# Output projection of a streaming-encoder block in a seven-product form, on eight cores

## The chip, the cores and the metric

One Trainium2 chip, all 8 of its cores, each working on its own eighth of the tokens. The metric is the device time of the slowest core in microseconds (us). A program on all eight cores has a second, slower state in some of its executions, in which the cores of a die show a lower granted clock of the matrix engine (TensorE); such runs are called slow here and are kept out of every comparison. A ratio sets the fast runs of one kernel against the fast runs of the kernel before, both taken in the same rounds on the same chip. It can differ by some 0.1% from the ratio of the means or medians of the times that are quoted.

## The reference

One layer: two token mixers side by side, one output projection of their joined outputs, then a squared-ReLU MLP of four times the width. D_MODEL is 1024, D_FF 4096, and there are 4 x 8192 tokens, so 4096 per core.

```python
def reference(x, ...):
    h = rmsnorm(x, norm1_g[l])
    p = jnp.einsum('bsd,de->bse', h, w_in[l])          # b_gate, c_gate, xc, u, v: 512 columns each
    # ... cut: mixer A, a gated width-3 convolution -> y_a ; mixer B, chunk-causal spatial gating -> y_b
    y = jnp.concatenate([rmsnorm(y_a, ...), rmsnorm(y_b, ...)], axis=-1)
    x = x + jnp.einsum('bse,ed->bsd', y, w_out[l])     # <- the output projection, 1024 x 1024
    h2 = rmsnorm(x, norm2_g[l])
    a = jax.nn.relu(jnp.einsum('bsd,df->bsf', h2, w_up[l]))
    x = x + jnp.einsum('bsf,fd->bsd', a * a, w_down[l])
    return rmsnorm(x, final_g)
```

## The kernel before

Each core handles eight tiles of MT = 512 tokens. The first stage ("mixing", about 70 to 430 us) goes through the eight tiles; the second ("expansion and contraction", 430 to 1220 us) runs the MLP on four groups of two tiles, with its weights streamed through six ring buffers. Between them lies what this text calls the passage: the last tile's mixing is interleaved with the first expansion matmuls. A small list scheduler in the kernel's own source orders all instructions of all engines when the program is built, from assumed costs, and the hardware then runs each engine's queue in that fixed order.

Expansion and contraction already use a seven-product (Strassen-Winograd) form: two halves of outputs by two halves of inputs by two halves of tokens take seven products instead of eight, for which sums of weights (on VectorE, "PREP" tiles, stored to DRAM during mixing) and sums of tokens are needed. The output projection did not: it took 8 groups of 8 matmuls of 512 columns a tile, and VectorE added each finished bank to the residual X.

```python
        def y_norm(src, q, ebase):               # YN: normalised mixer outputs, fp16, [8 x 128 inputs, 512 tokens]
            rs = RS[nxt("rs", 3)]
            rstd(rs[:, :], stats(src, q, 4, ONESE), MT, rs.keys())
            for c in (0, 2):
                tt(YN[:, ebase + c:ebase + c + 2, :], src[:, c:c + 2, :], rs[...].broadcast_to(...), ALU.mult, ...)

        def out_proj(m):
            b = X[(m + 1) % 3]
            for dc in range(8):
                bank = bank8()
                for e0 in (0, 4):
                    pe(bank, [(bank[:, :], WO[:, e_, dc * 128:(dc + 1) * 128], YN[:, e_, :], e_ == 0, e_ == 7)
                              for e_ in range(e0, e0 + 4)], YN.keys(e0, 4) + WO.keys(0, 8))
                tt(b[:, dc, :], bank[:, :], b[:, dc, :], ALU.add, bank.keys() + b.keys(dc), b.keys(dc))
                if dc % 2:                       # store two finished rows of the residual
                    ...
            rs = RS[nxt("rs", 3)]                # norm factors of the sum, stored for the MLP
            rstd(rs[:, :], stats(b, X1Q, 8, ONESD), MT, rs.keys())
            dma("sp", rs_d[m], rs[:, :], rs.keys(), ...)

        # ... cut: the order of a tile
            y_norm(YA, SQ[0], 0)
            if last:
                h2_part(0, 1)                    # MLP inputs H of tile 1 (the first group is tiles 0 and 1), and sums
                h2_sums()
                refill(4)                        # first loads of MLP weights into the ring
            for c in range(4):
                stage_su(m, c)                   # gating
```

Of the kernel before, what the change touches and what calls it, by code (L numbers as in the profile page):

```python
# [17 lines left out]
MT = 512  # L18
# [48 lines left out]
class Sched:  # L67
# [44 lines left out]
    def schedule(self, phys, rounds=8):  # L112


        base = [(op, op.deps) for op in self.ops]
        best = None
        for _ in range(rounds + 1):
            for op, deps in base:
                op.deps = deps
                for b in op.banks:  # L120
                    b.left = len(b.ops)
            order = self.place([op for op, _ in base], phys)
            est = max(o.finish for o in order)
            if best is None or est < best[0]:
                best = (est, order, [(o, o.deps) for o in order],
                        [(o.opens, o.opens.phys) for o in order if o.opens is not None],
                        {o: (o.start, o.finish) for o in order})
            self.push(order, est)
        self.est_total, self.ops = best[:2]
        for o, deps in best[2]:  # L130
            o.deps = deps
            o.start, o.finish = best[4][o]
        for b, p in best[3]:
            b.phys = p
        self.by_eng = {e: [o for o in self.ops if o.eng == e] for e in ENGS}
# [42 lines left out]
    def place(self, ops, phys, lat=0.12, dma_lat=2.0, dma_rate=290e3):  # L178
# [67 lines left out]
        assert len(order) == len(ops)  # L246
# [73 lines left out]
def build_program():  # L320
# [23 lines left out]
    with es:  # L344
# [23 lines left out]
        SQ = [ar.buf(f"SQ{i}", (o + 68 + 4 * i) * KB, [4, MT], BF16) for i in range(2)]  # L368
        HT = [ar.buf("HT0", (o + 126) * KB, [8, MT], F16), ar.buf("HT1", (o + 76) * KB, [8, MT], F16)]
        PREP = [ar.buf(f"PREP{i}", (o + 84 + 7 * i) * KB, [7, 4, 128], F16) for i in range(2)]  # L370
        VH = ar.buf("VH", (o + 98) * KB, [4, MT], F16)
        CT = [ar.buf(f"CT{i}", (o + 102 + 2 * i) * KB, [MT], F32) for i in range(2)]
        T2 = [ar.buf(f"T2{i}", (o + 106 + 2 * i) * KB, [MT], F32) for i in range(2)]
        X = [ar.buf(f"X{i}", (o + a) * KB, [8, MT], F32) for i, a in enumerate((134, 110, 150))]
        WO = ar.buf("WO", (o + 166) * KB, [8, 1024], F16)
        YN = ar.buf("YN", (o + 182) * KB, [8, MT], F16)
        RS = [ar.buf(f"RS{i}", (o + 190 + 2 * i) * KB, [MT], F32) for i in range(3)]
        XQ = [ar.buf("XQ0", (o + 126) * KB, [8, MT], BF16), ar.buf("XQ1", (o + 76) * KB, [8, MT], BF16)]
        X1Q = ar.buf("X1Q", (o + 182) * KB, [8, MT], BF16)
# [8 lines left out]
        RSL = [ar.buf(f"RSL{i}", (o + 196 + 2 * i) * KB, [MT], F32) for i in range(2)]  # L388
# [7 lines left out]
        HQ = [ar.buf("HQ0", (o + 106) * KB, [8, HW], BF16), ar.buf("HQ1", (o + 108) * KB, [8, HW], F16)]  # L396
        SQH, HH = HQ[0][:, :, :], HQ[1][:, :, :]
        WSB = [ar.buf(f"WSB{i}", (o + 84 + 2 * i) * KB, [MT], F32) for i in range(3)]
# [30 lines left out]
        def act(out, in_, func, reads, writes, n=MT, **kw):  # L429
            aps = sum(1 for v in kw.values() if not isinstance(v, (int, float)))  # L430
            S.add("act", lambda e: e.activation(out=out, in_=real(in_), func=func, **kw), reads=reads, writes=writes,  # L431
                  occ=(n / 1.2 + 200 + 70 * aps) / 1000, banks=[in_.bank] if isinstance(in_, Late) else [])

        def dve(fn, reads, writes, n=MT, rate=1, src=None):
            S.add("dve", fn, reads=reads, writes=writes, occ=(n / rate + 151) / 960,
                  banks=[src.bank] if isinstance(src, Late) else [])
# [71 lines left out]
        def stage0_norm(m, bank, step=4):  # L508
            rs = RS[nxt("rs", 3)]
            rstd(rs[:, :], bank, MT, rs.keys())  # L510
            for k in range(0, 8, step):
                normalize(HT[m % 2], X[(m + 1) % 3], rs, k, step)
# [35 lines left out]
        def stage_conv(m, c):  # L548
# [7 lines left out]
            ct = CT[nxt("ct", 2)]  # L556
            act(ct[:, :], bC[:, :], AF.Identity, bC.keys(), ct.keys())
            tt(Z[:, c, 128:640], bX[:, :], ct[:, :], ALU.mult, bX.keys() + ct.keys(), Z.keys(c))
# [7 lines left out]
        def stage_su(m, c):  # L566
            h = HT[m % 2]
            bS, bU = bank8(), bank8()
            pe(bS, [(bS[64 * hh:64 * hh + 64, t * 128:(t + 1) * 128],
                     VH[:, t, (2 * c + hh) * 64:(2 * c + hh + 1) * 64], WST[:, 2 * c + hh, :], True, True)  # L570
                    for t in range(4) for hh in range(2)], VH.keys(0, 4) + WST.keys(0, 8))
            pe(bU, [(bU[:, :], WU[:, k, c * 128:(c + 1) * 128], h[:, k, :], k == 0, k == 7) for k in range(8)],
               h.keys(0, 8) + WU.keys(0, 8))
            t2 = T2[nxt("t2", 2)]
            bias_b = BIAS[:, c, :].unsqueeze(1).broadcast_to([128, 4, 128])
            stt(t2[:, :].rearrange("p (t i) -> p t i", t=4), bS[:, :].rearrange("p (t i) -> p t i", t=4),
                pcol(GLN, c), bias_b, ALU.mult, ALU.add, bS.keys() + [("BIAS",)] + CONST, t2.keys())
            tt(YB[:, c, :], bU[:, :], t2[:, :], ALU.mult, bU.keys() + t2.keys(), YB.keys(c))

        def y_norm(src, q, ebase):  # L580
            rs = RS[nxt("rs", 3)]
            rstd(rs[:, :], stats(src, q, 4, ONESE), MT, rs.keys())
            for c in (0, 2):
                tt(YN[:, ebase + c:ebase + c + 2, :], src[:, c:c + 2, :],
                   rs[:, :].unsqueeze(1).broadcast_to([128, 2, MT]), ALU.mult, src.keys(c, 2) + rs.keys(),
                   YN.keys(ebase + c, 2), n=2 * MT)

        def out_proj(m):
            b = X[(m + 1) % 3]
            for dc in range(8):  # L590
                bank = bank8()
                for e0 in (0, 4):
                    pe(bank, [(bank[:, :], WO[:, e_, dc * 128:(dc + 1) * 128], YN[:, e_, :], e_ == 0, e_ == 7)
                              for e_ in range(e0, e0 + 4)], YN.keys(e0, 4) + WO.keys(0, 8))
                tt(b[:, dc, :], bank[:, :], b[:, dc, :], ALU.add, bank.keys() + b.keys(dc), b.keys(dc))
                if dc % 2:
                    j = dc // 2
                    dst = x1_d[m, :, 2 * MT * j:2 * MT * (j + 1)].rearrange("p (k t) -> p k t", k=2)
                    dma("sp", dst, b[:, 2 * j:2 * j + 2, :], b.keys(2 * j, 2), [("x1", m, j)], ("xs", (m + 1) % 3, j),
                        4 * 128 * 2 * MT)  # L600
            rs = RS[nxt("rs", 3)]
            rstd(rs[:, :], stats(b, X1Q, 8, ONESD), MT, rs.keys())
            dma("sp", rs_d[m], rs[:, :], rs.keys(), [("rsd", m)], ("rss", m % 2), 4 * 128 * MT)

        def combine(p, dst, src, dkeys, reads, margin):
# [4 lines left out]
            tt(p[:, 4, :, :], p[:, 3, :, :], p[:, 2, :, :], ALU.add, p.keys(2, 2), p.keys(4), rate=2)  # L610
            tt(p[:, 3:6:2, :, :], p[:, 0:1, :, :].broadcast_to([128, 2, 4, 128]), p[:, 3:5, :, :], ALU.subtract,
               p.keys(0) + p.keys(3, 2), p.keys(3) + p.keys(5), n=1024, rate=2)
            tt(p[:, 6, :, :], p[:, 1, :, :], p[:, 5, :, :], ALU.add, p.keys(1) + p.keys(5), p.keys(6), rate=2)
# [5 lines left out]
        def prep(i, n):  # L619
            combine(PREP[n % 2], ws(i), wup_d if i < 16 else wdn_d, (i, ("pl", n % 2), ("ps", n % 2)), WO.keys(4) if n < 2 else [], 5.0)  # L620
# [99 lines left out]

        def down_unit(o_, s0, s1):
            bA, bC, bD = banks_acd()

# [11 lines left out]
            d1, d2 = o_, o_ + 4  # L735
            prod(bA, P1, True, False)
            addr(0, d1, bA)
            prod(bD, P2, True, True)
            addr(0, d1, bD)
            prod(bC, P5, True, False)  # L740
            addr(1, d2, bC)
            prod(bA, P6, False, False)
            addr(1, d1, bA)
            prod(bC, P3, False, True)
            addr(1, d1, bC)
            prod(bA, P7, False, False)
            addr(1, d2, bA)
            prod(bA, P4, False, True)
            addr(0, d2, bA)

        def final(g):

            rss = []
            for h in range(2):
                b, rs = R[h], RS[nxt("rs", 3)]
# [99 lines left out]
        for j in range(2):  # L855
            wload(WO[:, 4 * j:4 * j + 4, :], wo_d[j].rearrange("p (k n) -> p k n", k=4), WO.keys(4 * j, 4), ("o", j),
                  2048 * KB)
            gain(lambda k_: WO[:, k_, :], WO, range(4 * j, 4 * j + 4), GCONV, 1024)
# [45 lines left out]
        for m in range(NMT):  # L904
# [16 lines left out]
            y_norm(YA, SQ[0], 0)  # L921
            if last:
                h2_part(0, 1)
                h2_sums()
# [5 lines left out]
            y_norm(YB, SQ[1], 4)  # L930
# [138 lines left out]
```

## Time and profile before

| | |
|---|---|
| time, median of 3 | 1246.82 us (1246.3 to 1248.05) |
| span of the slowest core (core 7) | 1244.9 us |
| TensorE busy / idle | 1209.6 / 35.3 us |
| VectorE busy | 893.4 us |

The head of the page of the kernel before, and its first part: busy time, share of the span and instructions of each engine (PE is TensorE, PEld its weight loads, DVE is VectorE, ACT is ScalarE).

```profile
span 1244.9 us, 18564 instructions; the slowest of 8 cores (1235.7 to 1244.9 us)
...
PE 1209.6 (97%) x5880; PEld 548.5 (44%) x5880; DVE 893.4 (72%) x1377; ACT 530.4 (43%) x905; POOL 86.0 (7%) x146
```

The table by stage (windows) of the kernel before. After the window in us come its length, the busy time of each engine with its number of instructions, then the granted clock, the busy share of the DMA engines and their rate.

```profile
core 7: us, PE busy (x) PEld busy (x) DVE busy (x) ACT busy (x) POOL busy (x), PEclk, DMA share, GB/s
80.00:120.00 40.00, 40.00 (x199) 18.04 (x197) 33.96 (x49) 23.73 (x42) 2.32 (x4) 1.00 0.69 173
120.00:160.00 40.00, 40.00 (x199) 18.06 (x197) 29.39 (x46) 21.25 (x36) 2.13 (x4) 1.00 0.75 192
...
360.00:400.00 40.00, 40.00 (x211) 18.03 (x210) 33.20 (x45) 18.65 (x37) 3.70 (x7) 1.00 0.64 179
400.00:440.00 40.00, 40.00 (x211) 18.01 (x209) 34.28 (x49) 16.44 (x25) 3.73 (x7) 1.00 0.84 266
440.00:480.00 40.00, 40.00 (x187) 18.10 (x186) 29.52 (x43) 24.31 (x40) 6.80 (x10) 1.00 0.70 215
480.00:520.00 40.00, 40.00 (x187) 18.14 (x186) 33.23 (x61) 13.23 (x24) 3.19 (x6) 1.00 0.92 210
```

TensorE works 40.00 of 40.00 us in all of these windows at a granted clock of 1.00: everything else is hidden behind it. The 35.3 us of idle time lie in the load ramp and in the tail.

### The profile page before, as it was taken

The numbers are of one execution on the slowest core, as the hardware profiler recorded it, in microseconds if no ns is written. First come the engines' busy times: TensorE is split into PE (matmuls) and PEld (weight loads), VectorE is DVE, ScalarE is ACT, GpSimd is POOL, SyncE is SP. The second block draws the span as 40 slices with busy tenths as digits, with TensorE's granted clock in tenths as the row PEclk, the third lists the DMA queues.
The fourth block names the chain that finished last, engine by engine and source line by source line (L and its number), as shares of the span: only waits on it lengthen the run. The fifth ranks groups of instructions, "written<-read, shape, count | busy, mean of one in ns | idle before, by whom it ended". The sixth has DMA issues, their size and how long they took to land.

```text
span 1244.9 us, 18564 instructions; the slowest of 8 cores (1235.7 to 1244.9 us)
## 1 busy us (share of the span) xinstructions
PE 1209.6 (97%) x5880; PEld 548.5 (44%) x5880; DVE 893.4 (72%) x1377; ACT 530.4 (43%) x905; POOL 86.0 (7%) x146
## 2 busy tenths in 40 slices
PE   5899999999999999999999999999999999999994
PEld 3444444444444444444444444444444444444442
DVE  2778687877878887658759737767846876855746
ACT  4544655536554356026127205317405406503524
POOL 0100000000001011000101200000110000110000
PEclk9899999999999999999999999999999999999998
DMA  8968688596675869975577764576984645985423
GB/s 185 171 148 232 167 228 231 148 245 175 179 220 153 279 213 207 237 266 176 169 260 228 262 212 162 211 237 177 295 272 148 216 165 182 279 271 177 149 90 135
DMA packets 55183, 253.81 MB, mean 204 GB/s; under 512 B 6192, under 2 KB 6320, under 8 KB 54832
## 3 DMA queue, kind: packets, MB, share of 16 engines
q1 hardware_dynamic: 35152, 180.27, 42.8%
q0 software_dynamic: 19936, 72.36, 25.3%
q8 instruction: 49, 0.80, 0.3%
q14 instruction: 46, 0.38, 0.1%
HBM read 211.71 MB, written 65.01 MB: 222 GB/s over the span
## 4 chain that ended last, share of the span: by engine, by line
PE 93%; DMA 5%; DVE 1%; issue 0%; SPq 0%; DVEq 0%; POOLq 0%
PE PS L424 93%; DMA WSB_109<-bsf 2%; DMA X_74<-xT 1%; DMA X_73<-xT 1%; DMA WV<-wv 1%; DMA WCXB_53<-wcxb 1%; DVE RA L439 0%; DVE RB L439 0%; SPq L450 0%; DVE WU L446 0%; DVEq L344 0%; DVE FSQ_102 L439 0%; DVE FSQ_101 L439 0%; DVE Z L439 0%; DVEq L284 0%
## 5 line engine op out<-in xcount | busy, mean ns | idle before, releaser
L439 DVE TENSOR_TENSOR RB<-PS,RB 128x512 f32<-128x512 f32 x128 | 87.4, 690 | 91.4 <-PE PS L424 88.9
L424 PE MATMUL PS<-YN,WO 128*128 128x512 f16 x512 | 113.8, 379 | 0.0
L439 DVE TENSOR_TENSOR RA<-PS,RA 128x512 f32<-128x512 f32 x96 | 66.1, 690 | 60.6 <-PE PS L424 59.2
L439 DVE TENSOR_TENSOR A_89<-A_89 128x512 bf16<-128x512 bf16 (+1 forms) x192 | 94.5, 508 | 8.2 <-ACT A_89 L431 3.6
L431 ACT ACTIVATE SN_92<-PS 128x512 f32<-128x512 f32 x63 | 37.4, 595 | 106.5 <-PE PS L424 104.7
L424 PEld LDWEIGHTS PS<-YN,WO 128*128 128x128 f16 x512 | 50.1, 98 | 60.4
L424 PE MATMUL PS<-A_89,RING_83 128*128 128x512 bf16 x308 | 76.1, 379 | 0.0
L424 PE MATMUL PS<-A_89,RING_85 128*128 128x512 bf16 x308 | 76.1, 379 | 0.0
L424 PE MATMUL PS<-A_89,RING_86 128*128 128x512 bf16 x308 | 75.8, 379 | 0.0
L424 PE MATMUL PS<-A_89,RING_84 128*128 128x512 bf16 x308 | 75.5, 379 | 0.0
L424 PE MATMUL PS<-H_96,RING_87 128*128 128x512 f16 x308 | 75.1, 379 | 0.0
L424 PE MATMUL PS<-H_96,RING_83 128*128 128x512 f16 x308 | 74.5, 379 | 0.0
L424 PE MATMUL PS<-H_96,RING_88 128*128 128x512 f16 x308 | 74.3, 379 | 0.0
L424 PE MATMUL PS<-H_96,RING_84 128*128 128x512 f16 x308 | 74.3, 379 | 0.0
L431 ACT ACTIVATE SN_90<-PS 128x512 f32<-128x512 f32 x66 | 39.2, 595 | 76.7 <-PE PS L424 75.6
L424 PE MATMUL PS<-A_89,RING_88 128*128 128x512 bf16 x280 | 69.4, 379 | 0.0
L424 PE MATMUL PS<-A_89,RING_87 128*128 128x512 bf16 x280 | 69.1, 379 | 0.0
L431 ACT ACTIVATE SN_93<-PS 128x512 f32<-128x512 f32 x64 | 38.2, 596 | 71.8 <-PE PS L424 71.3
L424 PE MATMUL PS<-H_96,RING_85 128*128 128x512 f16 x280 | 67.9, 379 | 0.0
L424 PE MATMUL PS<-H_96,RING_86 128*128 128x512 f16 x280 | 67.4, 379 | 0.0
L431 ACT ACTIVATE SN_91<-PS 128x512 f32<-128x512 f32 x63 | 37.5, 595 | 70.1 <-PE PS L424 68.0
L439 DVE TENSOR_TENSOR SN_92<-PS,SN_92 128x512 f32<-128x512 f32 x63 | 43.4, 690 | 27.4 <-PE PS L424 22.7
(231 smaller groups left out, 2029.2 us busy)
## 6 DMA issues: line engine op xcount, KB each, us to landing
RING_83<-ws_s SPq DMA_DIRECT2D x21, 896.0 KB, 6.0
RING_84<-ws_s SPq DMA_DIRECT2D x21, 896.0 KB, 6.4
RING_87<-ws_s SPq DMA_DIRECT2D x20, 896.0 KB, 5.3
RING_88<-ws_s SPq DMA_DIRECT2D x20, 896.0 KB, 6.2
RING_85<-ws_s SPq DMA_DIRECT2D x19, 896.0 KB, 6.0
RING_86<-ws_s SPq DMA_DIRECT2D x19, 896.0 KB, 6.3
ws_s<-PREP_65 SPq DMA_DIRECT2D x12, 896.0 KB, 6.3
ws_s<-PREP_66 SPq DMA_DIRECT2D x12, 896.0 KB, 5.6
```

Of the source, the lines that this page charges most:

```text
L424: ins = e.matmul(real(o_), lhsT=l, rhs=r, start=st, stop=sp, skip_group_check=True)
L431: S.add("act", lambda e: e.activation(out=out, in_=real(in_), func=func, **kw), reads=reads, writes=writes, occ=(n / 1.2 + 200 + 70 * aps) ...
L439: dve(lambda e: e.tensor_tensor(out=out, in0=real(in0), in1=in1, op=op), reads, writes, n, rate, in0)
```

## The change

The output projection takes the seven-product form too, over halves of outputs (512), of inputs (512, which are the two mixers) and of the tile's tokens (256). A product is 4 x 2 matmuls of 256 columns, and two 128-wide output chunks share a bank of 512. That makes 2 x 7 x 8 = 112 matmuls of 256 columns a tile instead of 64 of 512: seven eighths of the arithmetic. Its cost: 14 additions of 2 x 256 columns a tile instead of 8 of 512, three sums over the tokens a tile, three sums over the weights once. Weights grow from 16 to 28 KB a partition, tokens from 8 to 14 KB; SBUF was full, so several buffers now lie on top of others. VH now shares memory with RSL, for which a part of the first MLP inputs H (those of tile 1, built during the last tile) comes after the gating instead of before it. The scheduler got a random search of 90 tries; it now assumes that VectorE and ScalarE are occupied for less time by an instruction, and that the result comes later. The diff, cut to its core:

```diff
-    def schedule(self, phys, rounds=8):
+    def schedule(self, phys, rounds=8, tries=90):
...
+            if t:
+                for o, k in best[5].items():
+                    o.key = k if o.fixed else k + rnd.gauss(0, 0.3)
...
-            S.add("dve", fn, reads=reads, writes=writes, occ=(n / rate + 151) / 960,
+            S.add("dve", fn, reads=reads, writes=writes, occ=(n / rate + 65) / 960,
+                  dur=(n / rate + 237) / 960, ...)
...
         def out_proj(m):
-            b = X[(m + 1) % 3]
-            for dc in range(8):
-                bank = bank8()
-                for e0 in (0, 4):
-                    pe(bank, [(bank[:, :], WO[:, e_, dc * 128:(dc + 1) * 128], YN[:, e_, :], e_ == 0, e_ == 7)
-                              for e_ in range(e0, e0 + 4)], YN.keys(e0, 4) + WO.keys(0, 8))
-                tt(b[:, dc, :], bank[:, :], b[:, dc, :], ALU.add, bank.keys() + b.keys(dc), b.keys(dc))
+            x = X[(m + 1) % 3]
+            half = MT // 2
+            for dc in (0, 2):
+                def prod(bank, p, first, last):
+                    a, b = p
+                    pe(bank, [(bank[:, half * u:half * (u + 1)], WO[:, a, k, (dc + u) * 128:(dc + u + 1) * 128],
+                               YN[:, b, k, :], first and u == 0 and k == 0, last and k == 3)
+                              for u in range(2) for k in range(4)],
+                       YN.keys(b) + WO.keys(a))
+                def add(h, d_, bank):
+                    v = x[:, d_:d_ + 2, half * h:half * (h + 1)]
+                    tt(v, bank[:, :].rearrange("p (u t) -> p u t", u=2), v, ALU.add, ...)
+                winograd(prod, add, dc)          # seven products, seven additions; a bank is added to again after it was read
...
-        RS = [ar.buf(f"RS{i}", (o + 190 + 2 * i) * KB, [MT], F32) for i in range(3)]
+        RS1 = [ar.buf(f"RS1{i}", (o + 104 + 2 * i) * KB, [MT], F32) for i in range(3)]
+        RS2 = [ar.buf(f"RS2{i}", (o + 190 + 2 * i) * KB, [MT], F32) for i in range(3)]
...
             y_norm(YA, SQ[0], (3, 2))
             if last:
-                h2_part(0, 1)
-                h2_sums()
                 refill(4)
             for c in range(4):
                 stage_su(m, c)
+            if last:
+                h2_part(0, 1)
+                h2_sums()
+            y_norm(YB, SQ[1], (4, 1))
+            tsum(lambda i, j, d: YN[:, i:j:d, :, :], lambda j: YN.keys(j), 2 * MT)
```

## The prediction

> **What bounds the kernel now.** TensorE. The 40 us windows of the slowest core (span 1244.9 us) show it busy 40.00 of 40.00 us in every window from 80 to 1200 us; its idle time (1244.9 - 1209.6 = 35.3 us) lies in the load ramp before about 69 us and the tail after 1227 us. The chain of waits is 93% matmuls. Granted clock is 1.00 from 80 to 1200 us. A matmul record lasts 379 ns but they are pipelined: 48 output-projection matmuls in a row took 10.52 us in the timeline, a step of (10520-379)/47 = 215.8 ns.
>
> **Removed.** 512 matmuls of 512 columns become 896 of 256 (7/8 of the arithmetic). The timeline has 52 warm-up matmuls of 128 columns, each with its own 128x128 weight load, in 3.07 us, 56 ns a step; a line through 56 ns at 128 and 215.8 at 512 gives 109 ns at 256 (an estimate). That agrees with the Trainium skill, "TensorE: Matmul & The Clock Gate", section "Wait — 56ns, not 53.3ns?": columns over 2.4 GHz plus about 2.5 ns. As weight loads hide even at 128 columns in this trace, twice as many should not show. 512 x 0.2158 = 110.5 us becomes 896 x 0.109 = 97.7 us: a gain of at most 12.8 us, all on the critical path.
>
> **Added, on VectorE.** Per tile 14 evictions of 2x256 instead of 8 of 512, 0.69 us each (+4.1 us), and three sums over the normalised tokens (1.22 + 0.69 + 0.69 = 2.6 us, from the same forms elsewhere): 6.7 us a tile, 54 us in all, plus some 5 us once for sums of weights. VectorE is busy 40.3 of 51 us a tile now; it would be 47.0 of about 49.5, 95% by durations, some 90% in truth, as back-to-back instructions start 0.08 us sooner than they last. It is not the bound, but a full in-order engine answers late, and the seven products chain: one bank is added to, read by VectorE, added to again, four times a unit. Two units side by side and convolution matmuls between them (the instruction order shows them) should hide most. I book 3 us of new TensorE idle: mostly the first two tiles (VectorE is at 85% from 80 to 120 us already), at most half a microsecond a tile after.
>
> **Moved.** Two scratch tiles go, buffers overlap more, the schedule is searched anew. The steady part has nothing to gain from that, ramp and tail perhaps 1 us either way. The expansion, contraction and final stages should stay the same.
>
> **Prediction.** 1246.8 - 12.8 + 3 = 1237 us (-0.8%), 8 in 10 between 1231 and 1247. Faster by over 2%: 1%. Within 2%: 95%. Slower by over 2%: 4%.
>
> **What would show it right or wrong.** 896 output-projection matmuls stepping at 109 ns in the timeline; weight-load time up by 384 x 98 ns = 38 us, harmless; VectorE busy +50 to +60 us, at 90 to 96% in the first 470 us; TensorE busy about 1197 us, idle about 38. Matmul waits for VectorE in the waits view: few, under 1 us each. The first expansion matmuls start about 10 us earlier.
>
> **What would make it wrong.** A 256-wide step well above 109 ns (at 123 ns the whole gain is gone): weight loads not hidden, or the two chunks of a bank not streaming freely. VectorE too late: 1.6 us of idle a tile takes all the gain. A slower ramp from the weight sums. On the other side, no stalls and a better ramp: 1232.

## More of the kernel before

Groups of instructions of the kernel before: name and shape, count, busy us and mean ns of one, then the idle time of the engine just before them and what ended it.

```profile
line engine op names shapes xcount | busy us, mean ns | idle before us <-releasers
L424 PE MATMUL PS<-YN,WO 128*128 128x512 f16 x512 | 113.8, 379 | 0.0
...
L424 PEld LDWEIGHTS PS<-YN,WO 128*128 128x128 f16 x512 | 50.1, 98 | 60.4
...
L439 DVE TENSOR_TENSOR X_73<-PS,X_73 128x512 f32<-128x512 f32 x24 | 16.6, 691 | 10.1 <-PE PS L424 10.0
L439 DVE TENSOR_TENSOR X_74<-PS,X_74 128x512 f32<-128x512 f32 x24 | 16.3, 688 | 8.4 <-PE PS L424 8.2
...
L439 DVE TENSOR_TENSOR X_72<-PS,X_72 128x512 f32<-128x512 f32 x16 | 11.0, 689 | 6.2 <-PE PS L424 6.1
```

The last three lines are the additions of projection banks to the residual. VectorE was idle for 10.1 + 8.4 + 6.2 = 24.7 us in front of them, waiting for TensorE: in 39 of the 64 cases (its list of waits counts 19 + 10 + 10) it stood ready when a bank was finished.

A line of TensorE's timeline in the kernel before (start, duration, ..., count):

```profile
397.53 13.98 PE L424 MATMUL PS<-YN,WO 128*128 128x512 f16 x64
```

A matmul record lasts 379 ns, but they are pipelined: the step is (13980 - 379)/63 = 215.9 ns.

Transfers of the kernel before issued from 400 to 490 us, the passage (names, issuing queue, count, KB each, median us from issue to landing):

```profile
XS_95<-x_s POOLq DMA_DIRECT2D x3, 512.0 KB, 6.3
...
ws_s<-PREP_66 SPq DMA_DIRECT2D x1, 896.0 KB, 8.9
...
RING_83<-ws_s SPq DMA_DIRECT2D x1, 896.0 KB, 4.7
...
rs_s<-RS_78 SPq DMA_DIRECT2D x2, 256.0 KB, 8.7
```

## The result, and the profile after

The changed kernel took 1251.93 and 1254.40 us in its two fast runs (three more were slow: 1273.23, 1280.09 and 1481.95), against a median of 1247.13 us before. The ratio of the fast runs is 1.0048, 95% interval 1.0024 to 1.0072. Four fast runs in a later round of runs gave 1.0050. The change costs half a per cent, where I had predicted a gain of 0.8%, and the time lies above the predicted range.

The head and first part of the page after (slowest core 3, span 1250.4 us):

```profile
span 1250.4 us, 19543 instructions; the slowest of 8 cores (1238.0 to 1250.4 us)
...
PE 1199.9 (96%) x6264; PEld 586.2 (47%) x6264; DVE 941.9 (75%) x1460; ACT 532.0 (43%) x905; POOL 87.7 (7%) x148
```

TensorE's busy time fell by 9.7 us and its idle time rose from 35.3 to 1250.4 - 1199.9 = 50.5 us, by 15.2 us. Together that is +5.5 us, the difference of the spans. The groups after, to be laid beside those of before:

```profile
L432 PE MATMUL PS<-YN,WO 128*128 128x256 f16 x896 | 105.6, 273 | 3.4 <-DVE SN_86 L448 1.4 <-ACT VH L439 1.3 <-DVE SN_87 L448 0.7
...
L432 PEld LDWEIGHTS PS<-YN,WO 128*128 128x128 f16 x896 | 87.1, 98 | 24.4 <-issue 5.8
...
L448 DVE TENSOR_TENSOR X_75<-PS,X_75 128x512 f32<-128x512 f32 x42 | 27.8, 685 | 1.8 <-PE PS L432 1.4
L448 DVE TENSOR_TENSOR X_76<-PS,X_76 128x512 f32<-128x512 f32 x42 | 27.4, 684 | 2.2 <-PE PS L432 1.9
...
L448 DVE TENSOR_TENSOR X_74<-PS,X_74 128x512 f32<-128x512 f32 x28 | 18.4, 684 | 0.8 <-PE PS L432 0.6
...
L448 DVE TENSOR_TENSOR YN<-YN 128x1024 f16<-128x1024 f16 x16 | 10.9, 682 | 0.0
...
L448 DVE TENSOR_TENSOR YN<-YN 128x2048 f16<-128x2048 f16 x8 | 9.7, 1216 | 0.0
```

The matmuls did what they should. A run of 56 of them in the timeline after

```profile
241.02 6.28 PE L432 MATMUL PS<-YN,WO 128*128 128x256 f16 x56
```

has a step of (6280 - 273)/55 = 109.2 ns, so 896 of them cost 97.8 us where 512 x 215.9 ns = 110.5 us were spent before: 12.7 us less. VectorE's added work came near the prediction too (VectorE busy +48.5 us). But VectorE's idle time in front of the additions shrank from 24.7 to 1.8 + 2.2 + 0.8 = 4.8 us, and it stood ready for a bank in 8 of 112 cases instead of 39 of 64. The banks themselves don't wait longer: with the additions paired in order with their products, a finished bank waited 1.27 us on average for its addition, against 1.55 us before. What shrank is the time that VectorE had to spare.

The same windows after:

```profile
80.00:120.00 40.00, 38.70 (x259) 22.54 (x258) 40.00 (x58) 21.89 (x34) 2.14 (x4) 1.00 0.70 188
120.00:160.00 40.00, 37.09 (x222) 21.71 (x221) 33.20 (x47) 21.61 (x39) 1.60 (x3) 0.96 0.66 164
...
360.00:400.00 40.00, 40.00 (x256) 22.28 (x254) 37.16 (x55) 18.58 (x35) 3.70 (x7) 1.00 0.84 190
400.00:440.00 40.00, 35.80 (x231) 19.95 (x231) 35.34 (x54) 18.45 (x29) 3.20 (x6) 1.00 0.97 287
440.00:480.00 40.00, 37.13 (x192) 18.74 (x190) 33.47 (x48) 21.34 (x34) 8.94 (x14) 0.96 0.87 241
480.00:520.00 40.00, 33.70 (x146) 14.73 (x147) 27.25 (x50) 11.09 (x19) 2.66 (x5) 0.91 0.86 201
```

TensorE loses 1.30 + 2.91 us from 80 to 160 us and 4.20 + 2.87 + 6.30 us from 400 to 520 us, 17.6 us together; from 160 to 400 us it loses nothing. (That this is more than 15.2 us comes from the ramp: up to 80 us TensorE was busy for 65.3 us here and for 61.0 us in the core shown before.) These are the slowest cores; over all eight, TensorE's idle time between 80 and 560 us is 0.7 us on average before and 13.7 us after. In three of those windows the granted clock falls as well, to 0.96, 0.96 and 0.91: the trace has it at half for 3.4 us from 128.6 and from 452.8 us and for 6.8 us from 483.6 us, each time from near the end of a wait on. From 480 to 520 us 146 matmuls took 33.70 us, 0.231 us each, against 187 in 40.00 us or 0.214 before: 2.5 us more for the same work. Such stretches at half the clock are, by estimate, why TensorE's busy time fell by 9.7 and not by 12.7 us.

The waits themselves, in TensorE's timeline after (the bracket holds the idle time just before, and what ended it):

```profile
84.31 1.91 PE L432 MATMUL PS<-YN,WO 128*128 128x256 f16 x16 [1.30 <-ACT VH L439]
...
129.06 1.01 PE L432 MATMUL PS<-SQ_61,ONESE 128*128 128x512 bf16 x2 [2.92 <-DVE SQ_61 L448]
...
424.01 0.59 PE L432 MATMUL PS<-SQ_61,ONESE 128*128 128x512 bf16 x2 [2.09 <-DVE SQ_61 L448]
...
434.82 1.03 PE L432 MATMUL PS<-YN,WO 128*128 128x256 f16 x8 [1.41 <-DVE SN_86 L448]
...
453.04 1.87 PE L432 MATMUL PS<-H_92,RING_79 128*128 128x512 f16 x4 [1.78 <-DVE X_76 L448]
...
486.00 1.86 PE L432 MATMUL PS<-H_92,RING_83 128*128 128x512 f16 x4 [6.63 <-ACT SN_87 L439]
```

Two of them show how they came about. VectorE's timeline shortly before the wait that ended at 424.01 us:

```profile
417.86 0.68 DVE L448 TENSOR_TENSOR YB<-PS,YB 128x512 f32<-128x512 f32 x1
421.91 0.75 DVE L451 SCALAR_TENSOR_TENSOR H_92<-XS_90,PRM,RSL_99 128x512 f16<-128x512 f32 x1 [3.37 <-DMA x_s<-X_75]
422.58 0.68 DVE L448 TENSOR_TENSOR YB<-PS,YB 128x512 f32<-128x512 f32 x1
```

VectorE works its queue in order. It stood for 3.37 us in front of a piece of the MLP input H, with a product of YB behind it; the profile puts this down to the store of a residual tile (x_s<-X_75), which had been issued at 407.56 us and took 14.25 us to land. In the layout of both kernels H lies on top of that residual buffer, so H waits until the store has read it. (The kernel before has such a wait too, of 2.3 us for x_s<-X_73, but TensorE lost nothing by it.) The statistics that TensorE needed at 424 us came two instructions after that. The Trainium skill says the same of this engine ("TensorE: Matmul & The Clock Gate", section "Architectural detail: the array is 16× 32×32, not 1× 128×128": ScalarE and VectorE are strict first in, first out), and this trace agrees. ScalarE before the wait that ended at 486.00 us:

```profile
485.26 0.60 ACT L439 ACTIVATE SN_87<-PS 128x512 f32<-128x512 f32 x1 [8.65 <-DMA rs_s<-RS_72]
```

It waited 8.65 us for the store of the last tile's norm factors (rs_s), because it was to write a scratch (SN_87) that in the new layout lies on top of them. And the transfers of 400 to 490 us were slow. After:

```profile
ws_s<-PREP_69 SPq DMA_DIRECT2D x2, 896.0 KB, 11.1
XS_91<-x_s POOLq DMA_DIRECT2D x3, 512.0 KB, 13.3
...
ws_s<-PREP_70 SPq DMA_DIRECT2D x1, 896.0 KB, 13.6
...
RING_83<-ws_s SPq DMA_DIRECT2D x1, 896.0 KB, 16.2
...
rs_s<-RS_72 SPq DMA_DIRECT2D x2, 256.0 KB, 15.9
```

Three stores of prepared weights (ws_s) now fall into the passage where one did, and the ring loads of 896 KB, of which one is shown, take 14.4 to 19.1 us to land instead of 4.5 to 6.5.

### The profile page after: what moved, and what is told of

It reads as the page before. It is cut to its first block, busy times and chain, and to the rows that moved or that the text cites. A ratio compares the mean times of both kernels' runs of the same rounds, so it can differ in the third digit from the quotient of the medians.

```text
span 1250.4 us, 19543 instructions; the slowest of 8 cores (1238.0 to 1250.4 us)
## 1 busy us (share of the span) xinstructions
PE 1199.9 (96%) x6264; PEld 586.2 (47%) x6264; DVE 941.9 (75%) x1460; ACT 532.0 (43%) x905; POOL 87.7 (7%) x148
## 4 chain that ended last, share of the span: by engine, by line
PE 85%; DMA 9%; DVE 3%; issue 2%; ACT 0%; DVEq 0%; SPq 0%; ACTq 0%; POOLq 0%
PE PS L432 85%; DMA X_75<-xT 2%; DMA rs_s<-RS_72 1%; DMA x_s<-X_75 1%; DMA XS_91<-x_s 1%; DMA oT<-RA 1%; DMA RA<-x_s 1%; DMA X_76<-xT 1%; DMA WCXB_51<-wcxb 1%; DMA WCXB_52<-wcxb 0%; DVE RA L448 0%; DVE RB L448 0%; DVE H_92 L451 0%; DVE A_85 L448 0%; DVE A_85 L451 0%
## 5 line engine op out<-in xcount | busy, mean ns | idle before, releaser
L432 PE MATMUL PS<-YN,WO 128*128 128x256 f16 x896 | 105.6, 273 | 3.4 <-DVE SN_86 L448 1.4
L432 PEld LDWEIGHTS PS<-YN,WO 128*128 128x128 f16 x896 | 87.1, 98 | 24.4 <-issue 5.8
L432 PE MATMUL PS<-H_92,RING_83 128*128 128x512 f16 x308 | 76.0, 382 | 6.6 <-ACT SN_87 L439 6.6
L432 PE MATMUL PS<-H_92,RING_79 128*128 128x512 f16 x308 | 77.2, 387 | 1.8 <-DVE X_76 L448 1.8
L432 PE MATMUL PS<-H_92,RING_80 128*128 128x512 f16 x308 | 75.2, 382 | 0.0
L432 PE MATMUL PS<-H_92,RING_84 128*128 128x512 f16 x308 | 74.6, 379 | 0.5 <-DVE X_76 L448 0.5
L432 PE MATMUL PS<-H_92,RING_81 128*128 128x512 f16 x280 | 68.3, 379 | 0.0
L432 PE MATMUL PS<-H_92,RING_82 128*128 128x512 f16 x280 | 68.3, 379 | 0.0
```

The costliest lines, as they stand in the source:

```text
L432: ins = e.matmul(real(o_), lhsT=l, rhs=r, start=st, stop=sp, skip_group_check=True)
```

## The experiments

There were eighteen runs: thirteen new kernels, four of them run twice, and the changed kernel again. "Wrong" marks those whose result is wrong. Those called "order unchanged" keep every instruction of every engine in the place it had; the diffs shown are shortened, and the bookkeeping that keeps the order is left out of them.

To see where a kernel gains or loses, I worked out from each profile's matmul records when TensorE had done 60,000, 600,000, 860,000 and 2,480,000 columns of matmul work outside the output projection, the small matmuls of the gating and the statistics (the whole is 2.49 million), each matmul counted once. The mean over the six of eight cores whose records are most complete is used, in us; sums are rounded by themselves. The first mark lies after the ramp, the second near the end of the seventh tile (379 to 390 us), the third behind the passage (518 to 544 us), the last near the end. Between kernels of one order all three stretches may be compared; between different orders only the sum of the first two, as a projection may stand before or behind a mark.

| kernel | ratio to before | 60k to 600k | 600k to 860k | sum | 860k to 2,480k |
|---|---|---|---|---|---|
| before | 1 | 336.1 | 141.7 | 477.9 | 685.6 |
| b1_fewer (order of before) | 0.9914 | 325.0 | 139.4 | 464.3 | 685.5 |
| b2_fewer_vector (order of before) | 0.9967 | 329.0 | 141.4 | 470.4 | 685.8 |
| b3_search_again | 1.0042 | 333.9 | 143.7 | 477.7 | 685.5 |
| after | 1.0048 | 329.1 | 150.9 | 479.9 | 689.0 |
| a1_after_again (order of after) | 1.0050 | 329.4 | 152.1 | 481.6 | 687.8 |
| a2_light_again (order of after) | 0.9981 | 329.0 | 147.0 | 476.0 | 688.0 |
| a3_rs_again (order of after) | 1.0016 | 329.3 | 147.5 | 476.8 | 688.1 |
| b4_both (order of after) | 0.9988 | 327.9 | 143.3 | 471.2 | 686.5 |
| c1_thin_again (order of after) | 0.9975 | 327.2 | 145.8 | 473.0 | 687.6 |
| c2_thin_both (order of after) | 0.9953 | 327.1 | 141.7 | 468.8 | 685.6 |
| c3_old_search | 1.0111 | 331.1 | 159.9 | 491.0 | 685.5 |

My first theory was that the passage is limited by transfers and takes back whatever TensorE brings to it. Rivals: VectorE's added work; the order and layout of the changed kernel; the scheduler's search and costs.

### First round of runs: e1 to e4

In these four runs the chip granted only about 0.945 of the clock even in fast runs (before: 1305 to 1311 us in fast runs), so the matrix work weighed more than usual and only ratios count.

**e1_thin_evict.** Order unchanged, wrong: each addition of the projection touches 2 x 2 columns instead of 2 x 256.

```diff
-                    tt(v, bank[:, :].rearrange("p (u t) -> p u t", u=2), v, ALU.add,
+                    tt(v[:, :, 0:2], bank[...].rearrange("p (u t) -> p u t", u=2)[:, :, 0:2], v[:, :, 0:2], ALU.add,
```

> The changed kernel with the same instruction order on every engine, but each of the 14 evictions of the output projection per tile adds 2x2 columns only (wrong result on purpose). That takes some 14 x 0.5 = 7 us of VectorE work out of each tile, more than the change added (6.7 us). Rival theory (VectorE is full and answers late): the TensorE idle of 70 to 560 us, some 7 to 17 us a core in the changed kernel, all but goes, VectorE-bound gaps near 84, 431-437 and 450-453 us vanish, and the fast time falls to 1238 to 1242 us. Main theory (at the change from mixing to the MLP, in-order VectorE and ScalarE queues stand before instructions that wait for stores to land): the fixed gaps near 431-453 us (4 us together) shrink, but the gaps near 424 and 480 us stay in most cores, and the time falls by 3 to 6 us only, to 1247 to 1250 us.

Measured: one fast run of four, 1294.60 us (the others 1359.64 to 1466.8), so no ratio. Waits for VectorE of 0.7 to 1.4 us were still there at the passage, and I took this as evidence against VectorE. That was a wrong reading: one run at an odd clock decides nothing, and a wait that is still there may have become shorter. The run was repeated later as c1.

**e2_light_loads.** Order unchanged, wrong: the first eight loads of MLP weights into the ring bring two of their seven parts, and the first expansion units use those parts.

```diff
-                dma("sp", RING[s][:, :, :, :], ws(i), ...)
+                q = 6 if n < 8 else 1
+                dma("sp", RING[s][:, ::q, :, :], ws(i)[:, ::q, :, :], ...)
```

> The changed kernel with the same instruction order, but the first eight weight loads of the MLP bring two of seven blocks (256 KB instead of 896 KB each, wrong result on purpose), so that the stores of the block input and of the norm factors compete with less traffic between 395 and 475 us. Main theory: the stores land in 5 to 8 us instead of 13 to 17, the gap near 424 us goes, the one near 480 us gets smaller, the gaps near 431-453 us stay; the fast time falls by 3 to 7 us, to 1246 to 1250 us. Rival (VectorE full): no change, 1252 to 1254 us.

Measured: ratio 0.9927 (0.9881 to 0.9974). The wait at 424 us was gone from all eight cores; the others mostly stayed (the one near 480 us was gone from three cores).

**e3_rs_moved.** Order unchanged, correct: the last tile's norm factors go to a buffer that nothing overlaps at that time.

```diff
             rs = RS1[nxt("rs", 3)]
+            if m == NMT - 1:
+                rs = RS2[2]
```

> The changed kernel with the same instruction order, right result; only the last tile's norm factors (2 KB) lie in a buffer that no MLP scratch overlaps, so that ScalarE need not wait for their store to land before it writes that scratch. If that overlap, new in this layout, makes the gap near 480 us (1 to 7 us in seven of eight cores), the gap goes and nothing else changes: the fast time falls by 2 to 6 us, to 1247 to 1251 us. If the gap has another cause (the bank, VectorE), it stays and the time is 1252 to 1254 us.

Measured: 0.9926 (0.9874 to 0.9978). The wait at 480 us was gone from all cores.

**e4_search_only.** The kernel before, with the changed kernel's search and costs; the projection stays in the old form. Correct.

> The kernel before with the changed kernel's schedule search (90 random tries) and instruction costs, but the plain output projection and the old buffers. If the search and its costs are what makes the order fragile, this one too shows TensorE idle of 5 us or more between 400 and 520 us and takes 1250 us or more. If the seven-product form with its buffers is needed for the loss, it is within 3 us of the kernel before (1244 to 1249 us) with almost no idle there. I expect the second, at 1246 us.

Measured: 0.9995 (0.9941 to 1.0048), no waits. At this clock.

### Second round of runs: the same at a normal clock, and a repair

**a1_after_again**, the changed kernel unaltered.

> The changed kernel unaltered, so that the others of this call stand beside it on one chip. On a chip like the first (clock 0.99) about 1.005 of the kernel before, with TensorE gaps near 84, 128, 424, 431-437, 450 and 480 us of 8 to 15 us together; on a chip like the last one (clock 0.945) between 0.993 and 1.000 of it, since slower matmuls hide the transfers better.

Measured: 1.0050 (1.0029 to 1.0071), with the same waits. The first round's ratios cannot be set beside the result of 1.0048: at the low clock the two kernels of e2 and e3 came out 0.5 and 0.9% lower against the kernel before than they do here (a2 and a3).

**a2_light_again**, as e2.

> Same kernel as e2_light_loads (same order as the changed kernel, the first eight MLP weight loads cut to 2 of 7 blocks, wrong result on purpose). If crowded transfers hold up the stores at the change of stage, it is 3 to 7 us faster than the changed kernel of this call and the gap near 424 us is gone on all cores; the gaps near 431-437 and 450 us (order of VectorE's work) stay. If VectorE alone is the cause, it is within 1 us of the changed kernel.

Measured: 0.9981 (0.9948 to 1.0014), 0.7% below a1. The table puts the gain into the passage (152.1 to 147.0 us).

**a3_rs_again**, as e3.

> Same kernel as e3_rs_moved (same order as the changed kernel, right result, the last tile's norm factors in a buffer that no MLP scratch overlaps). The gap near 480 us is gone and the time is 2 to 5 us under the changed kernel of this call.

Measured: 1.0016 (0.998 to 1.0052), about 0.3% below a1, which is not clear of the noise (a1's interval begins at 1.0029). The wait for the norm factors was gone from all cores, but waits of 0.6 to 5.0 us for ring loads appeared at 478 to 513 us in most.

**f1_margins.** An attempt to repair the passage, correct: norm factors moved, one RSL buffer moved so that tile 1's H can be built before the last tile's gating again, and the scheduler told to expect 6 to 7 us more for the two stores in question.

```diff
-            rs = RS1[nxt("rs", 3)]
+            rs = RS1[nxt("rs", 3)] if m < NMT - 1 else RS2[2]
+        RSL1G0 = ar.buf("RSL1G0", (o + 40) * KB, [MT], F32)     # used for group 0
+            ... margin=6.0 (residual stores), margin=7.0 (norm-factor stores); h2_part and h2_sums back before the gating
```

> The changed kernel with four edits at the change of stage: the last tile's norm factors in a buffer of their own; the norm factors of tile 1 in a buffer that does not lie under the gating input, so that the MLP input of tile 1 is again made before the gating of the last tile, as in the kernel before; and the scheduler told that stores of the block input land 6 us, of the norm factors 7 us later than the default says. The seven-product form and its VectorE work are untouched. If the loss is the wait on transfers at the change of stage, TensorE idle between 400 and 520 us falls under 3 us a core and the time is 10 to 16 us under the changed kernel of this call and 8 to 13 us under the kernel before (0.990 to 0.994). If VectorE's load is the cause, it is within 3 us of the changed kernel.

Measured: 1.0050 (1.0013 to 1.0088). A clear miss. Four of the waits vanished, and all eight cores got a new one of 3.4 to 11.1 us for ring loads at about 500 us. New order, new wait: this spoke for the transfers, and against mending waits one at a time.

### Third round of runs: the saving alone, VectorE alone, the search alone

**b1_fewer.** The kernel before, order unchanged, wrong: one of the eight matmuls of a projection group is left out. This takes about as much TensorE work away as the change does (64 x 215.9 ns = 13.8 us), and adds nothing.

```diff
-            for (o_, l, r, st, sp) in mms:
+            for (o_, l, r, st, sp) in mms[:len(mms) - leave]:
```

> The kernel before, every order on every engine unchanged, but of the eight output-projection products of each group the last is left out (wrong result on purpose): 64 matmuls of 512 columns less, 64 x 215.8 ns = 13.8 us of TensorE work, a little more than the change saves; VectorE, buffers and transfers as in before. Theory J (the passage from mixing to expansion is limited by transfers, whatever form the projection has): TensorE comes to it some 10 us early and waits there, waits of 4 to 10 us for VectorE or DMA between 400 and 520 us, ratio to before 0.994 to 0.998. Rival O (the saving is usable, and what eats it in the changed kernel is its own order and layout: late halves of the sums, reused scratch, later weight preparation): no waits over 2 us after 80 us, ratio 0.988 to 0.991.

Measured: 0.9914 (0.9894 to 0.9934), 10.7 us by the ratio; by the table all of it (464.3 against 477.9 us). Only three cores had a wait at the passage, about 3 us each for ring loads. My first theory had asked for 0.994 to 0.998 and fell: the passage does not take back what TensorE brings to it. (Rival O's band of 0.988 to 0.991 with no wait over 2 us is just missed too.) The slowest core gains less than the mean core because the waits left are unevenly spread.

**b2_fewer_vector.** The same, and ten times a tile VectorE does an addition of 480 columns into a scratch of its own just before an addition or normalisation of the projection.

```diff
+            def fn(e):
+                e.tensor_tensor(out=SPARE[:, :, :], in0=BIAS[:, :, 0:120], in1=BIAS[:, :, 0:120], op=ALU.add)
+                return e.tensor_tensor(out=out, in0=real(in0), in1=in1, op=op)
```

> As the run with fewer products, and ten times a tile VectorE does one more addition of 480 columns (into a scratch of its own) just before an eviction or a normalisation of the projection: about 0.65 us each, 6.5 us a tile, as much as the change adds; order otherwise unchanged. Theory J and rival O: the same as the run without it within 0.2% (VectorE has room in the middle tiles). Rival V (a full VectorE eats the saving): at least 5 us slower than the run without it, with TensorE waits for VectorE in the tiles.

Measured: 0.9967 (0.995 to 0.9983), 6.6 us above b1, for 52.3 us of added VectorE time (80 instructions of 654 ns). No other queue was altered. The rival of the full VectorE, which had asked for at least 5 us, is confirmed: on average one us lost for eight us of VectorE work, though VectorE is nowhere busy all the time. Core 2 from 80 to 120 us, b1 and then b2:

```profile
80.00:120.00 40.00, 39.90 (x209) 17.96 (x209) 35.28 (x49) 23.05 (x43) 1.06 (x2) 1.00 0.88 182
```

```profile
80.00:120.00 40.00, 37.56 (x178) 16.57 (x179) 36.72 (x53) 23.27 (x41) 1.52 (x3) 0.96 0.74 196
```

TensorE loses 2.34 us more in b2, where VectorE is busy 36.72 of 40 us, and a line of core 0's timeline in b2 shows what for: a sum of squares whose halves VectorE added up late. The same matmuls waited 2.2 to 2.6 us in all eight cores (in cores 2 and 4 the profile names ScalarE's YA as what ended the wait). Smaller waits follow in every core: some 1.0 us near 156 us, 0.6 to 0.9 us near 354 us, and 1.3 and 1.05 us for ScalarE at the passage.

```profile
109.77 0.59 PE L428 MATMUL PS<-X1Q,ONESD 128*128 128x512 bf16 x2 [2.17 <-DVE X1Q L443]
```

**b3_search_again**, as e4.

> The kernel before with the changed kernel's search of the schedule and its costs of instructions, the eight-product form kept; run before at a low clock (0.9995 of before), now at a normal one, I hope. Theories J and O: within 0.3% of before, no waits over 3 us after 80 us. Rival S (search and costs alone make the waits): ratio 1.004 or more with waits at 400 to 520 us.

Measured: 1.0042 (1.0022 to 1.0062), with waits of 1.1 to 4.9 us for VectorE at about 493 us in five cores. At a normal clock the searched order does harm the old form. I had expected no effect.

**b4_both.** The changed kernel's order, norm factors moved and ring loads light together; wrong.

> The changed kernel's order, with both earlier single changes at once: the last tile's norm factors moved to their own buffer, and the first eight ring loads brought down to two of seven parts (wrong result on purpose). If the loss lies at the passage from mixing to expansion: waits for the norm factors and for ring loads gone together, some 2 to 4 us of waits left there, ratio to before 0.992 to 0.996, that is 10 to 13 us below the changed kernel. If the loss lies mostly elsewhere (first tiles, expansion, clock): the two gains do not add, ratio 0.998 or more.

Measured: 0.9988 (0.9961 to 1.0015), which lies in the second band: little more than nothing, and no better than the light loads alone. In the profiled run the mean core was better (8.8 us less in the passage than a1), but single cores still had waits of 2 to 4 us for ring loads, and the slowest core counts. Taking these two waits away does not bring the saving back; the waits of 1.2, 0.7 and 1.8 us for VectorE at 426 to 451 us stayed in all eight cores.

### Fourth round of runs: which part of the changed kernel

**c1_thin_again**, as e1 at a normal clock.

> The changed kernel, order unchanged, each of the 14 additions of a tile's projection reading and writing 2x2 columns instead of 2x256 (wrong result on purpose): some 0.45 us each, 6 us of VectorE work a tile less, which is what the change had added. Tried before at a low clock with one fast run only. If VectorE's load eats the gain (rival V, as the run with fewer products and a loaded VectorE suggests): 5 to 8 us below the changed kernel, ratio to before 0.998 to 1.001 or lower, TensorE at 385 us ahead by 10 to 12 us instead of 7. If it does not: ratio 1.003 to 1.007 as the changed kernel.

Measured: 0.9975 (0.9959 to 0.9991), 0.75% or 9.3 us below the changed kernel (a1, on another chip: two ratios are compared, give or take some 3 us), slightly past the expected 5 to 8. VectorE's busy time is that of the kernel before again, with all of the change's transfers, layout and order in place:

```profile
PE 1195.6 (96%) x6264; PEld 585.7 (47%) x6264; DVE 890.4 (72%) x1460; ACT 531.5 (43%) x905; POOL 88.2 (7%) x148
```

The table says where: against a1 2.2 us in the first seven tiles, 6.3 us in the last tile and the passage. At the second mark, near 380 us, TensorE is 9.7 us ahead of the kernel before (mean of all eight cores), where I had asked for 10 to 12, and 6.3 us in a1. The wait at 424 us is gone from seven of eight cores though no transfer was altered: an earlier VectorE stores earlier, and the loads that follow are earlier too. So the passage's waits for transfers were partly VectorE's lateness in another form. A thin addition also frees its bank sooner for the next product of the chain; c1 does not tell this from VectorE's load, but b2, which has no such chain, lost 6.6 us by load alone.

**c2_thin_both.** c1 and b4 together; wrong.

> The same with the norm factors of the last tile in their own buffer and the first eight ring loads light (wrong result on purpose). If VectorE's load and the passage together are all of the loss: ratio 0.991 to 0.994, as the run of before with fewer products. If something else is in it (searched order, spread between cores): 0.995 or more.

Measured: 0.9953 (0.9928 to 0.9978). That misses the band of "VectorE and passage are all of it" (0.991 to 0.994) and lies just inside that of "something else". By the table the mean core does the first two stretches in 468.8 us, 9.1 less than before, so most of the 12.7 is there; the slowest core does not get it all, with waits of 1 to 5.5 us for ring loads in six cores. And four waits stay in every core that none of these runs removed: 1.30 us near 84 us for ScalarE (VH), and 0.79, 0.70 and 1.40 us for VectorE (SN, SN and X) between 424 and 447 us, 4.2 us in all. Neither b1 nor the undisturbed cores of h7 below have them.

**c3_old_search.** The change without the search and with the old costs. Correct.

```diff
-    def schedule(self, phys, rounds=8, tries=90):
+    def schedule(self, phys, rounds=8, tries=0):
```

(and the two cost lines of the change's diff undone)

> The change with the scheduler's search switched off and its old costs of VectorE and ScalarE instructions; form, buffers and sums of the change kept; correct result. If the searched order is a large part of the loss (as its 1.0042 on the kernel before suggests): 3 to 6 us below the changed kernel, ratio 1.000 to 1.003. If form and layout make the loss: 1.004 or more.

Measured: 1.0111 (1.0092 to 1.0129), the opposite of my expectation. For the seven-product form the search gains 0.6%, though it costs 0.4% on the old form. The searched order as such is not the cause.

**c4_old_search_rs.** The same with the norm factors moved.

> The same with the last tile's norm factors in their own buffer, order scheduled anew; correct result. If search and overlap both count: 6 to 9 us below the changed kernel, ratio 0.997 to 1.000, and the wait for the norm factors at 480 us gone. If not: as the run without it.

Measured: two fast runs of eight, 1257.12 and 1260.44 us, no ratio. Inconclusive; no sign of a gain over c3's 1257 to 1264 us.

### Fifth round of runs: a kernel that keeps the form only where VectorE has room

**h7_last_plain.** The last tile goes back to the eight-product form, for which one subtraction restores the overwritten quarter of the weights; norm factors moved; scheduled anew with the search. Correct.

```diff
+            for dc in range(8) if m in EIGHT else ():            # EIGHT = {7}
+                bank = bank8()
+                for y, a in ((2, (0, 3)[dc // 4]), (0, (1, 2)[dc // 4])):
+                    pe(bank, [(bank[...], WO[:, a, k, dc % 4 * 128:(dc % 4 + 1) * 128], YN[:, y:y + 2, k, :],
+                               y == 2 and k == 0, y == 0 and k == 3) for k in range(4)], ...)
+                tt(x[:, dc, :], bank[:, :], x[:, dc, :], ALU.add, ...)
+            for dc in (0, 2) if m not in EIGHT else ():
...
+            if m == NMT - 2:
+                tt(WO[:, 3, :, :], WO[:, 0, :, :], WO[:, 3, :, :], ALU.subtract, ...)
-            rs = RS1[nxt("rs", 3)]
+            rs = RS1[nxt("rs", 3)] if m < NMT - 1 else RS2[2]
```

> The changed kernel, last tile's norm factors in their own buffer, and the last of the eight tiles projected in the old eight-product form (no sums over its tokens, 8 evictions of 512 instead of 14 of 2x256; one subtraction restores the fourth quarter of the weights after the seventh tile); scheduled anew with the search; correct result. It gives up 1.6 us of the TensorE saving. If VectorE's load in the last tile is worth about 5 us: 3 to 6 us below the changed kernel, plus what the moved norm factors are worth (3 to 5), ratio 0.995 to 1.000. If it is not: 1.001 or more.

Measured: 0.9947 (0.9929 to 0.9965), four fast runs of 1237.41 to 1241.09 us; the other four were slow. This correct kernel beats both: 0.5% under before, 1.0% under the changed kernel. Its profile fell in the slow state, but cores 2 to 5 were undisturbed (spans 1232.7 to 1239.1 us). Core 3 of it, at the passage:

```profile
400.00:440.00 40.00, 39.98 (x187) 17.96 (x185) 36.91 (x52) 18.47 (x31) 3.18 (x6) 1.00 0.96 298
440.00:480.00 40.00, 37.82 (x168) 16.61 (x167) 27.49 (x41) 23.12 (x39) 7.84 (x12) 0.96 0.90 235
480.00:520.00 40.00, 38.67 (x179) 17.27 (x178) 29.17 (x55) 6.43 (x11) 2.11 (x4) 1.00 0.90 223
```

TensorE loses 3.5 us here where the changed kernel lost 13.4. The order is new, so this run alone does not separate the lighter VectorE from the moved norm factors and the order itself; c1 and a3 vary the first two with the order kept. The additions of that core:

```profile
L448 DVE TENSOR_TENSOR X<-PS,X 128x512 f32<-128x512 f32 x106 | 69.6, 684 | 4.7 <-PE PS L432 4.4
```

VectorE has as little time to spare in front of them as in the changed kernel (4.7 against 4.8 us), and yet little of its lateness reaches TensorE.

**h07_ends_plain.** The first tile in the old form too, the sums of weights made after it.

> The same with the first tile in the old form too, and the sums over weights made after it instead of in the ramp; correct result. The first tile costs another 1.6 us of saving and gives back 2 to 3 us: the same as the run with only the last tile plain, within 0.3%, ratio 0.994 to 1.000. If the seven-product form loses where VectorE is full and nowhere else, TensorE has no wait over 1 us between 80 and 400 us here.

Measured: one fast run of eight, 1247.15 us, no ratio. Its undisturbed cores had waits of 2.4 to 5.2 us for ring loads at 484 to 491 us and of up to 1.6 us for H at 430. Between 80 and 400 us no core had a wait of 1 us, as expected. Inconclusive on the time, and no better than the run above.

## Why the prediction was wrong, point by point

- **TensorE as the bound, and the step of a 256-wide matmul: right.** 109 ns predicted, 109.2 measured; 12.7 us less in that group. The rule that the prediction cites held.
- **Weight loads hidden: right.** Their time rose by 37.7 us (38 predicted), and the step did not suffer.
- **Added VectorE work: nearly right in size.** 48.5 us against 50 to 60. VectorE is busy 33.2 to 40.0 of 40 us in the mixing windows, 83 to 100% where 90 to 96% was said.
- **"I book 3 us of new TensorE idle: mostly the first two tiles ..., at most half a microsecond a tile after": this is the step that failed.** New idle time was 15.2 us, and the lower clock after the waits cost about 3 us more (the 12.7 us less of matmul work, against 9.7 us less of busy time). The first two tiles lost 4.2 us, near the 3 booked, which is luck in part: 1.3 us of it, the wait near 84 us, is there in c1 too, with VectorE's additions thinned. The middle tiles lost nothing. The last tile and the passage lost 13.4 us, for which I had booked half a microsecond. I had looked at VectorE's load in the average tile, and not at the last one, where it also builds the first MLP inputs and, in order, stands before stores that have to land first, and where its own lateness makes those stores late. The runs show it twice: VectorE work alone, added to the kernel before, costs 6.6 us (b2 against b1), and taken out of the changed kernel, order kept, gives back 9.3 us (c1 against the changed kernel). It is not all: in c1 the mean TensorE idle time between 80 and 560 us is still 8.9 us of the 13.7.
- **"Moved ... nothing to gain", "ramp and tail perhaps 1 us either way", "The expansion, contraction and final stages should stay the same": wrong in the passage.** I noted that buffers overlap more and did not ask what the new overlap makes wait. The norm factors under the MLP scratch cost 8.65 us of waiting on ScalarE in one core, and moving them is worth about 0.3% (a3), which is within the noise. The search is not neutral either: -0.6% on this form, +0.4% on the old.
- **"The first expansion matmuls start about 10 us earlier": 6 us, and of no use.** They start at 417 to 429 us in the eight cores after (423.3 on average), at 426 to 434 us before (429.3). The waits of the passage then took more than that back.
- **What would make it wrong: named, with a wrong distribution.** "VectorE too late: 1.6 us of idle a tile takes all the gain" names the cause; it came in two places and not in each tile.

In sum, the saving of 12.7 us was had and more than spent. Of what c1 and c2 give back in the ratios, 9.3 us are VectorE's additions, and about 2.7 us more the two waits at the passage once VectorE is out of the way; this second figure is not clear of the noise. These shares depend on each other: light loads alone gave some 8 us (a2 against a1), moved norm factors 4 (a3), thinned additions 9.3 (c1), and all three together 12 (c2).

Still open: why the slowest core lies further above the mean core in the changed kernel (1253.6 against 1244.8 us in a1's fast runs; 1247.3 against 1241.3 before, in the same round); the 2 to 3 us that the changed kernel loses after 860,000 columns, where single cores wait for R tiles or ring loads; how much of the slow transfers is due to the later weight preparation, which no run varied by itself; and what makes the four waits that c2 keeps in every core. Their 4.2 us are about the size of the 0.4% by which c2 stays above b1, but no run took them away with the order kept. Half or more of the runs of some changed kernels were slow; no experiment touched why.

## What to carry to other kernels

Removing work from the bound engine in exchange for work on an engine that is "only" 80% busy is not free: look at how often that engine stands ready for the results it has to pick up (39 of 64 additions before, 8 of 112 after). A small number is a warning and not a forecast, as the last kernel shows, which gains with 4.7 us of idle time there. What counts is which late answers reach the bound engine. Do the sum for the busiest tile and for the change of stages, not for the average tile, and for each new overlap of buffers ask what will wait for what. A faster form may pay in some tiles and not in others: keeping it in seven of eight, with one buffer moved and a new order, turned +0.5% into -0.5%.

## What the Trainium skill lacked or had wrong

- "TensorE: Matmul & The Clock Gate", section "Back-to-back issue gap", gives a sustained roofline of about 131 ns for a matmul of 512 columns in a stream of weight loads and matmuls, and says that columns over 2.4 GHz plus 2.5 ns over-counts there. Here such a stream stepped at 215.9 ns at 512 columns and 109.2 ns at 256, each with its own 128x128 weight load of 98 ns: the formula held and the roofline did not. Its table entry of 262 cycles for 256 columns agrees.
- The same page, section "Seeing it yourself", says to budget 1.95 GHz, on the default power profile, for sustained dense matmuls on all cores (which profile was set here is not on record). In the fast runs here the mean granted clock was 0.98 to 0.99 of full speed on all eight cores, about 0.945 in one round of runs; a clock of about 0.81 was seen only in slow runs, and there on one die (0.81 to 0.82 on cores 4 to 7 in the run of 1481.95 us).
- "DMA: Bandwidth & Descriptors", section "Latency and other measured facts", puts the fixed cost of a DMA at about 2 us. I found no page that says what a transfer takes when several queues are full: here an 896 KB ring load (RING_83) landed in 4.7 us before, issued at 450.9 us with a DMA share of 0.70 (440 to 480 us), and in 16.2 us after, issued at 422.0 us with a share of 0.97 (400 to 440 us).
- I found no page that gives the price of a late VectorE for TensorE below saturation. Here 52.3 us of added VectorE work cost 6.6 us of time (b2 against b1) at a VectorE load of 32.8 to 36.7 of 40 us in the windows from 80 to 200 us (core 2 of b2).
